# Seven-multiplication projections of a macaron decoder block: products that add up in one PSUM bank, two column pairs in alternation, and another order of pools

## Chip, cores and metric

The kernel runs on one core of a Trainium2 chip, as one launch. The metric is the device time of an execution in microseconds; lower is better. The profile is taken of one execution, with the time of every instruction on TensorE (PE), VectorE (DVE), ScalarE (ACT), GpSimd (POOL) and of the DMA issues on SyncE (SP).

## What is computed

A decoder block over 1024 positions of width 1024, all in float32: a SwiGLU feed-forward stage with half weight, a token mixer, a second feed-forward stage, a final norm. Cut to what matters here:

```python
def swiglu(h, w_in, w_out):
    a, b = jnp.split(h @ w_in, 2, axis=-1)          # 1024 x 1024 by 1024 x 5632
    return (jax.nn.silu(a) * b) @ w_out             # 1024 x 2816 by 2816 x 1024

h = rms_norm(x, norm_ffn1[l]) * (1.0 + sc1) + sh1
x = x + FFN_RESIDUAL * g1 * swiglu(h, ffn1_w_in[l], ffn1_w_out[l])
h = rms_norm(x, norm_mix[l]) * (1.0 + sc2) + sh2
x = x + g2 * token_mixer(h, ..., mix_w_in[l], ...)   # begins with h @ mix_w_in
h = rms_norm(x, norm_ffn2[l]) * (1.0 + sc3) + sh3
x = x + FFN_RESIDUAL * g3 * swiglu(h, ffn2_w_in[l], ffn2_w_out[l])
```

The shifts, scales and gates come from nine modulation vectors, each a product of the conditioning vector with a 1024 x 1024 block of `ada_w`.

## The kernel before

**Matmuls.** A float32 operand is kept as two float32r tiles, a high part (`parts`: an ACT cast, L90) and a low part (a subtraction, L91, on DVE or, for the first weights of a stage, on POOL). A product term is three matmuls of 128 x 128 by 128 x 512: high by high, high by low, low by high (`mmw`, L232 to L234).

**Seven products.** `paired` (L242) computes the projections h @ w_in of the two FFN stages (20 iterations each) and part of that of mix (14 iterations). An iteration takes one pair of column blocks. The weights form a 2 x 2 block matrix (a11, a12 in the tile `ra`, a21, a22 in `rb`), the activations another (b11, b21, b22 and the sums t1 to t4, made once per stage on POOL). Seven block products of 12 matmuls each (`product`, L298) take the place of eight; sums and differences of weights are formed on DVE in `prepare` (L302) and split into the operands w11, w12, w22, ws1 to ws4 in the pool `wp`, 11 tiles. `prepare` of an iteration runs during the iteration before. The pools `hq` and `bq` hold t2, t3 and t4, `hp` the other operands.

Each of the seven products has a PSUM bank of its own, in turn from the pools `pa` and `pb` (four banks each). ACT copies the first bank to a tile (L321); DVE adds the others onto it in seven additions (L323 to L335), in tiles of the pool `cq` ("c"). `emit` follows for each half: `swiglu` in the FFN stages (an ACT Silu and a DVE product), `mix_in` in mix.

**Around it.** In FFN1 `between` (L741) computes the modulation vectors for later: four per iteration in 14 iterations, each a load of 512 KB (`ada`, through the pool `rp` of three buffers, which `ra` and `rb` use too) and a DVE instruction of 128 x 1024 (L154). In both FFN stages `combos` forms the operands of the second product from finished pairs and stores them to DRAM (`bd`, L369).

**Second product.** After `paired`, `ffn` multiplies by w_out, again with seven products, each over eleven blocks and four banks (L432). An operand comes from DRAM: a load into `br` (L404), a cast and a split into `ob`; the weights come through `ar` and `oa`. The pools of this stage (`s1q`, `s2q`, `uq`, `oa`, `ob`, `br`, L393) take the space that `wp` and the others of `paired` have left, in the order in which they are named; so a tile's first writer waits for the last reader of what lay there. The tiles of the following stage of mix (its `wp`, then a unit's weights `wh` and `wl`, L93 to L98) in turn lie on those.

The order on each engine follows the priorities of a tile scheduler: program order, shifted by `defer`. Each engine takes its instructions in that order and waits in place. PE runs the products of an iteration in program order. The change to `paired` starts at L260:

```python
self.part(ctx, wp=11, hq=8, bq=4)
```

Of the kernel before, what the change touches and what calls it, by code (L numbers as in the profile page):

```python
# [22 lines left out]
NKK = 11  # L23
# [17 lines left out]
class Block:  # L41
# [19 lines left out]
    @contextmanager  # L61
    def defer(self, n):

        keep = self.tc.cur_priority
        self.tc.cur_priority = keep + n
        yield
        self.tc.cur_priority = keep

# [160 lines left out]
    def mmw(self, ps, w, i, x, first, last):  # L229
        wh, wl = w[:, 0, i * P:(i + 1) * P], w[:, 1, i * P:(i + 1) * P]  # L230
        mm = self.nc.tensor.matmul
        mm(ps, wh, x[:, 0, :], start=first, stop=False)  # L232
        mm(ps, wh, x[:, 1, :], start=False, stop=False)  # L233
        mm(ps, wl, x[:, 0, :], start=False, stop=last)  # L234
# [7 lines left out]
    def paired(self, ctx, h, hctx, src, order, warm, emit, after, right, ready=()):  # L242


        nc = self.nc
# [4 lines left out]
        def tt(dst, a, b):  # L250
            V.tensor_tensor(dst, a, b, op=sub)
# [8 lines left out]
        self.part(ctx, wp=11, hq=8, bq=4)  # L260
# [26 lines left out]
        for i in range(4):  # L287
            x11, x12, x21, x22 = h[0][i], h[1][i], h[0][4 + i], h[1][4 + i]
            for o, x, y in ((x11, x12, x11), (x12, x22, x12), (x22, x22, x11), (x21, x21, x22)):
                nc.gpsimd.tensor_tensor(o, x, y, op=sub)  # L290
            t2.append(hq(x22))
            t3.append(hq(x12))
            t1.append(self.parts(x11))
            t4.append(self.parts(x21, self.bq, "bq"))
# [18 lines left out]
        ops = None  # L313
        for n, f in enumerate(order):
            if f not in fs:
                w11, w12, w22, ws1, ws2, ws3, ws4 = ops if ops else prepare(f)
                ops = prepare(order[n + 1]) if n + 1 < len(order) else None
                p1, p2, p3, p4, p5, p6, p7 = [self.acc() if (7 * n + i) % 2 == 0 else self.bank() for i in range(7)]
                product(p1, w11, b11)
                c11, c21, c22, u = (self.piece() for _ in range(4))  # L320
                A.copy(u, p1)  # L321
                product(p2, w12, b21)
                V.tensor_tensor(c11, p2, u, op=add)  # L323
                product(p3, ws2, t2)
                V.tensor_tensor(u, p3, u, op=add)
                product(p4, ws3, t3)
                V.tensor_tensor(c22, p4, u, op=add)
                product(p5, w22, t4)
                V.tensor_tensor(c21, p5, c22, op=add)
                emit(f, 0, c11, c21, c21)  # L330
                product(p6, ws1, t1)
                V.tensor_tensor(c22, p6, c22, op=add)
                V.tensor_tensor(u, p6, u, op=add)
                product(p7, ws4, b22)
                V.tensor_tensor(u, p7, u, op=add)  # L335
                emit(f, 1, u, c22, c22)
            after(n, f)
# [6 lines left out]
    def ffn(self, h, hctx, w_in, w_out, gate, warm, residual, norm, done, between=None):  # L344
# [6 lines left out]
        gs = {f: [] for f in order}  # L351
# [4 lines left out]
        def swiglu(f, hh, a, b, dst):  # L356
            s = self.half()
            if dst is None:
                dst = self.half()
            A.activation(s, a, AF.Silu)  # L360
            V.tensor_tensor(dst, b, s, op=ALU.mult)
            gs[f].append(dst)

        def combos(i):

            (x11, x12), (x21, x22) = gs[i], gs[NKK + i]
# [12 lines left out]
            put(6, c4)  # L379
# [12 lines left out]
        with ExitStack() as ctx:  # L392
            self.part(ctx, s1q=11, s2q=11, uq=4, oa=4, ob=3, br=5)  # L393
            self.part(rctx, right=True, xp=8)
            xt, xs = self.xtiles()
            for hh in range(2):
                for i in range(4):
                    nc.sync.dma_start(xt[hh][i], residual(hh, i))
# [47 lines left out]
            b = product(self.acc, lambda i: block(i, 0), 0)  # L446
            us = []
# [227 lines left out]
    def run(self):  # L675
# [113 lines left out]
        def mix_in(f, hh, x, y, dst):  # L789
            sx = x if dst is not None else self.half()  # L790
            A.activation(sx, x, AF.Sigmoid)
            if f >= NH:
                sy = y if dst is not None else self.half()
# [3 lines left out]
            elif f in CONV_EARLY:  # L797
                if hh == 0:
                    us[f] = self.role("u")
# [220 lines left out]
```

## Time and profile before

| quantity | before |
|---|---|
| time, three runs | 2473.93, 2474.76 (median), 2480.92 us |
| profiled execution | 2474.77 us, span of its instructions 2473.0 us |
| PE busy | 2411.6 us, 98% of the span |
| DVE busy | 2012.1 us, 81% |
| ACT busy | 943.4 us, 38% |
| POOL busy | 115.9 us, 5% |
| mean granted PE clock | 0.994 of full speed |
| HBM | 266.31 MB read, 78.12 MB written |

Stages of the span: FFN1's paired stage ends at 484 us and its second product at 700; the first part of mix ends at 1014, the mixer's further parts at about 1810; FFN2's paired stage ends at 2245. A busy time counts instructions that execute; matmuls overlap, so the time between two starts, not the length of one, is what a matmul costs. "idle before <-X" on a row is the time for which the engine stood still ahead of it and what ended that. A window's row gives its length, the busy time of PE, PEld (PE's weight loads), DVE, ACT and POOL in that stretch, with their instructions, and the granted clock (1.00 is 2.4 GHz, 0.50 is 1.2 GHz).

### The profile page before, as it was taken

How to read it: one execution, taken by the hardware profiler on the slowest of the kernel's cores; microseconds unless marked ns; L12 is line 12 of the kernel's file. 1: busy time of each engine (PE TensorE's matmuls, PEld its weight loads, DVE VectorE, ACT ScalarE, POOL GpSimd, SP SyncE). 2: the span in 40 equal slices, each digit the busy share in tenths (PEclk: the TensorE clock that was granted, in tenths of full speed). 3: DMA queues.
4: the chain of work that ended last, by engine and by line, in shares of the span. 5: the costliest groups of instructions: out<-in, count | busy, mean ns of one | idle time of the engine just before them, and what ended most of it. 6: DMA issues, size and time to landing. Idle time of an engine off the chain costs nothing.

```text
span 2473.0 us, 30875 instructions
## 1 busy us (share of the span) xinstructions
PE 2411.6 (98%) x11320; PEld 2002.2 (81%) x11320; DVE 2012.1 (81%) x3010; ACT 943.4 (38%) x1679; POOL 115.9 (5%) x77
## 2 busy tenths in 40 slices
PE   4999999999999999999999999999999999999997
PEld 2788878888878888788888888888888888888886
DVE  8989899678889999799999877575668777775977
ACT  4522233344644333333333335453343333324443
POOL 3300000000060000000000000000050000000000
PEclk9999999999999999999999999999999999999999
DMA  7256565595523323211111112674523233328743
GB/s 276 67 189 209 196 208 187 175 340 179 168 85 119 107 78 113 94 64 61 60 43 64 56 56 82 232 265 157 159 81 124 90 107 106 103 86 291 273 130 124
DMA packets 139975, 346.46 MB, mean 140 GB/s; under 512 B 15536, under 2 KB 15664, under 8 KB 139824
## 3 DMA queue, kind: packets, MB, share of 16 engines
q1 hardware_dynamic: 139680, 343.97, 41.3%
q8 instruction: 89, 1.46, 0.2%
q10 hardware_dynamic: 144, 0.52, 0.1%
q14 instruction: 62, 0.51, 0.1%
HBM read 266.31 MB, written 78.12 MB: 139 GB/s over the span
## 4 chain that ended last, share of the span: by engine, by line
PE 90%; DVE 6%; DMA 2%; issue 1%; ACT 1%; POOL 0%; SPq 0%; DVEq 0%; ACTq 0%
PE pa L233 10%; PE pa L234 10%; PE pa L232 10%; PE pb L234 10%; PE pb L233 10%; PE pb L232 9%; PE pa L106 8%; PE pa L104 8%; PE pa L105 8%; PE pb L577 4%; DMA ada<-in_ada_w_dram 1%; DVE ada L154 1%; PE pb L616 1%; PE pb L601 1%; PE pb L636 1%
## 5 line engine op out<-in xcount | busy, mean ns | idle before, releaser
L90 ACT CAST w<-ra 128x512 fp32r<-128x512 f32 x402 | 238.4, 619 | 435.6 <-PE pb L234 120.0
L104 PE MATMUL pa<-h,wh 128*128 128x512 f32 x896 | 355.4, 397 | 1.5 <-ACT wh L90 1.5
L106 PE MATMUL pa<-h,wl 128*128 128x512 f32 x896 | 353.7, 395 | 1.8 <-DVE wl L91 1.8
L105 PE MATMUL pa<-h,wh 128*128 128x512 f32 x896 | 353.1, 394 | 0.0
L543 DVE SCALAR_TENSOR_TENSOR uc<-u,par,uc 128x1023 f32<-128x1023 f32 (+14 forms) x240 | 303.2, 1263 | 2.7
L91 DVE TENSOR_TENSOR w<-ra,w 128x512 fp32r<-128x512 f32 x378 | 255.0, 690 | 10.6 <-ACT w L90 9.4
L232 PE MATMUL pa<-h,w 128*128 128x512 f32 x504 | 198.4, 396 | 5.0 <-ACT h L90 3.4
L234 PE MATMUL pb<-h,w 128*128 128x512 f32 x504 | 198.0, 393 | 4.7 <-POOL w L91 4.7
L233 PE MATMUL pa<-h,w 128*128 128x512 f32 x504 | 199.2, 395 | 2.7 <-DVE h L91 2.7
L234 PE MATMUL pa<-h,w 128*128 128x512 f32 x504 | 198.1, 393 | 0.0
L106 PEld LDWEIGHTS pa<-h,wl 128*128 128x128 f32 x896 | 168.6, 188 | 36.2 <-DVE wl L91 2.5
L233 PE MATMUL pb<-h,w 128*128 128x512 f32 x504 | 197.5, 392 | 0.0
L104 PEld LDWEIGHTS pa<-h,wh 128*128 128x128 f32 x896 | 168.7, 188 | 35.3 <-ACT wh L90 2.3
L232 PE MATMUL pb<-h,w 128*128 128x512 f32 x504 | 196.3, 390 | 0.0
L105 PEld LDWEIGHTS pa<-h,wh 128*128 128x128 f32 x896 | 168.9, 188 | 33.1 <-issue 0.7
L90 ACT CAST ob<-br 128x512 fp32r<-128x512 f32 x154 | 95.7, 622 | 186.2 <-PE pb L234 80.1
L90 ACT CAST wh<-raw 128x1024 fp32r<-128x1024 f32 x80 | 84.0, 1052 | 207.2 <-PE pa L105 194.4
L91 DVE TENSOR_TENSOR ob<-br,ob 128x512 fp32r<-128x512 f32 x154 | 106.7, 694 | 64.8 <-ACT ob L90 64.1
L233 PE MATMUL pa<-ob,oa 128*128 128x512 f32 x352 | 137.4, 390 | 1.3 <-DVE ob L91 1.3
L232 PE MATMUL pa<-ob,oa 128*128 128x512 f32 x352 | 137.0, 389 | 0.0
L234 PE MATMUL pa<-ob,oa 128*128 128x512 f32 x352 | 137.0, 389 | 0.0
L360 ACT ACTIVATE s<-c 128x512 f32<-128x512 f32 x80 | 50.6, 633 | 186.1 <-DVE c L335 128.3
(233 smaller groups left out, 5035.2 us busy)
## 6 DMA issues: line engine op xcount, KB each, us to landing
ra<-in_ffn_w_in_dram SPq DMA_DIRECT2D x88, 512.0 KB, 4.2
br<-bd SPq DMA_DIRECT2D x154, 256.0 KB, 3.1
bd<-c SPq DMA_DIRECT2D x146, 256.0 KB, 2.0
ada<-in_ada_w_dram SPq DMA_DIRECT2D x72, 512.0 KB, 4.5
ar<-in_ffn_w_out_dram SPq DMA_DIRECT2D x88, 256.0 KB, 4.5
ra<-in_mix_w_in_dram SPq DMA_DIRECT2D x32, 512.0 KB, 3.7
raw<-in_mix_w_in_dram SPq DMA_DIRECT2D x32, 512.0 KB, 3.5
ar<-in_ffn_w_out_dram SPq DMA_DIRECT2D x22, 512.0 KB, 5.2
```

The lines of the kernel that those rows point to most:

```text
L90: self.nc.scalar.copy(hi, src)
L91: (eng or self.nc.vector).tensor_tensor(lo, src, hi.bitcast(F32), op=ALU.subtract)
L104: mm(ps, wh, x[:, 0, :], start=first, stop=False)
L105: mm(ps, wh, x[:, 1, :], start=False, stop=False)
L106: mm(ps, wl, x[:, 0, :], start=False, stop=last)
L154: self.nc.vector.scalar_tensor_tensor(raw, raw, 1.0, self.cs, op0=ALU.mult, op1=ALU.mult, accum_out=dst)
L232: mm(ps, wh, x[:, 0, :], start=first, stop=False)
L233: mm(ps, wh, x[:, 1, :], start=False, stop=False)
L234: mm(ps, wl, x[:, 0, :], start=False, stop=last)
L360: A.activation(s, a, AF.Silu)
L543: V.scalar_tensor_tensor(uc[:, j:], u[:, :S - j], cw(KC - 1 - j), uc[:, j:], op0=ALU.mult, op1=ALU.add)
L577: mm(ps[:, i * 64:(i + 1) * 64], ch(k, i), two(ch(qa, i))[:, :, 1, :], start=True, stop=True)
```

## The change

- `paired`: two iterations are interleaved. A bank `chain` takes w11 b11, then ws2 t2, then (during the next iteration) ws3 t3 and w22 t4, each product added on top of what is there; ACT copies the bank's state after the first (p1) and the second (u2). A bank `low` takes ws1 t1 (copied as p6), then ws4 b22. A bank `left` takes w12 b21. Three DVE additions are left: c11 = left + p1, c12 = low + u2, c22 = chain + p6; the fourth output is read from `chain` itself by `emit`. In the last iteration the order ends with ws4, ws3 (`third`), w12 (`second`), w22 (`fourth`).
- Pools: `wp` has 9 tiles, w22 a pool of 2 of its own; the t's are made in the order t1, t2 and t3, t4; `prepare` makes its operands in another order.
- `ffn`: the pools of the second product are opened in the order `uq, br, ob, s2q, oa, s1q`; the residual x is loaded after the first of its seven products.
- `gs` holds the halves by index, and `mix_in` reuses `y` as the place of its sigmoid only for the second half.

```diff
-        self.part(ctx, wp=11, hq=8, bq=4)
+        self.part(ctx, wp=9, w22=2, hq=8, bq=4)
...
-        def product(ps, w, xs):
-            for i in range(4):
-                self.mmw(ps, w, i, xs[i], i == 0, i == 3)
+        def product(ps, w, xs, more=False):
+            for i in range(4):
+                self.mmw(ps, w, i, xs[i], not more and i == 0, i == 3, more)
 
         def prepare(f):
...
-            w11, w12, w22 = wop(a11), wop(a12), wop(a22)
+            w11, w22 = wop(a11), self.parts(a22, self.w22, "w22")
             V.tensor_tensor(a22, a21, a22, op=add)
+            ws1, w12 = wop(a22), wop(a12)
             tt(a21, a11, a21)
             tt(a11, a22, a11)
+            ws2 = wop(a11)
             tt(a12, a12, a11)
-            ws2, ws3, ws1, ws4 = wop(a11), wop(a21), wop(a22), wop(a12)
+            ws4, ws3 = wop(a12), wop(a21)
...
+        def up(dst, src):
+            with self.sooner(200):
+                A.copy(dst, src)
+
+        def third(chain, ws3, t3, p6, c12, c22, f):
+            product(chain, ws3, t3, True)
+            with self.sooner(200):
+                V.tensor_tensor(c22, chain, p6, op=add)
+            emit(f, 1, c12, c22, c22)
+
+        def fourth(chain, w22, c11, n, f):
+            product(chain, w22, t4, True)
+            emit(f, 0, c11, chain, c11)
+            after(n, f)
...
-                p1, p2, p3, p4, p5, p6, p7 = [self.acc() if (7 * n + i) % 2 == 0 else self.bank() for i in range(7)]
...
+            def second():
+                left = self.bank()
+                product(left, w12, b21)
+                V.tensor_tensor(c11, left, p1, op=add)
+
+            product(chain, w11, b11)
+            up(p1, chain)
+            if old:
+                third(*old[0])
+            product(low, ws1, t1)
+            up(p6, low)
+            if not last:
+                second()
+            product(chain, ws2, t2, True)
+            up(u2, chain)
+            if old:
+                fourth(*old[1])
+            product(low, ws4, b22, True)
+            V.tensor_tensor(c12, low, u2, op=add)
+            old = (chain, ws3, t3, p6, c12, c22, f), (chain, w22, c11, n, f)
+            if last:
+                third(*old[0])
+                second()
+                fourth(*old[1])
...
-            self.part(ctx, s1q=11, s2q=11, uq=4, oa=4, ob=3, br=5)
+            self.part(ctx, uq=4, br=5, ob=3, s2q=11, oa=4, s1q=11)
```

How the instructions stand, at three places. The order of SP where FFN1's paired stage gives way to the second product, before (`ar` are loads of w_out, `br` loads of the stored operands, `bd` stores of them; behind a row, the semaphores that it waits for):

```order
L409 DMA ar_709_4228<-in_ffn1_w_out_dram 128x512 [waits DMAHW1_49,DVE_49]
L404 DMA br_675_4035<-bd00_210 128x512 [waits DMAHW2_49,PE_49]
L404 DMA br_679_4057<-bd01_211 128x512 [waits DMAHW3_49]
L369 DMA bd110_231<-c_646_3882 128x512 [waits DMAHW4_49,DVE_49]
L404 DMA br_683_4079<-bd02_212 128x512 [waits DMAHW5_49]
```

and with the change:

```order
L447 DMA ar_694_4256<-in_ffn1_w_out_dram 128x512 [waits DMAHW5_49,PE_49]
L410 DMA bd210_242<-c_606_3765 128x512 [waits DMAHW6_49,DVE_49]
L442 DMA br_636_3951<-bd00_210 128x512 [waits DMAHW7_49,PE_49]
L442 DMA br_640_3973<-bd01_211 128x512 [waits DMAHW0_49]
L410 DMA bd510_275<-c_612_3894 128x512 [waits DMAHW1_49,DVE_49]
```

The first `br` load waits for a count of PE's matmuls in both; before it is that of the end of the product of w22, the fifth of the last iteration's seven, now that of the end of `second`, the last but one. The loads behind it follow on the same queue.

The order of DVE at the end of mix's paired stage, before (L335 is the last addition of the stage, `msk` are the masks of the units to come, `wl` is the low part of a unit's weight):

```order
L335 TENSOR_TENSOR c_1397_8301<-pb_1393_8285,c_1397_8301 128x512
L828 CAST msk_8431<-rawmask_8432 128x128
L830 CAST msk_8431<-rawmask_8432 128x512 x5
L91 TENSOR_TENSOR wl_1420_8488<-raw_1418_8485,wh_1419_8487 128x1024
```

and with the change (L373 is c12, L335 c22, L358 c11 of `second`):

```order
L373 TENSOR_TENSOR c_1335_8135<-pb_1330_8130,c_1334_8134 128x512
L335 TENSOR_TENSOR c_1336_8136<-pa_1329_8129,c_1332_8132 128x512
L358 TENSOR_TENSOR c_1333_8133<-pb_1337_8237,c_1331_8131 128x512
L95 TENSOR_TENSOR wl_1361_8367<-raw_1359_8364,wh_1360_8366 128x1024
L95 TENSOR_TENSOR wl_1366_8429<-raw_1364_8426,wh_1365_8428 128x1024
L869 CAST msk_8310<-rawmask_8311 128x128
L871 CAST msk_8310<-rawmask_8311 128x512 x5
```

The first two `wl` stand ahead of the masks now, and behind the addition of `second`, the last product but one. On ACT, the cast of the first `wh` waits for the last product before, and for that of ws4 now.

The order of ACT where FFN1's second product ends and mix begins, before (`oa`, `ob` are operands of that product, `w` those of mix's first pair, `s` squares for the norm of the second half):

```order
L90 CAST oa_1040_5890<-a12_1039_5887 128x512
L90 CAST w_1049_5962<-ra_1047_5958 128x512
L90 CAST ob_1042_5895<-br_1041_5893 128x512
L90 CAST w_1050_5965<-ra_1047_5958 128x512
L90 CAST w_1051_5968<-ra_1048_5960 128x512
L90 CAST w_1052_5971<-ra_1048_5960 128x512
L90 CAST w_1055_5978<-ra_1053_5974 128x512
L90 CAST w_1056_5981<-ra_1053_5974 128x512
```

and with the change:

```order
L94 CAST ob_1003_5819<-br_1002_5817 128x512
L214 ACTIVATE s_1025_5932<-x_626_3938 128x512
L214 ACTIVATE s_1026_5935<-x_626_3938 128x512
L214 ACTIVATE s_1027_5938<-x_627_3939 128x512
L94 CAST w_1011_5889<-ra_1009_5885 128x512
L94 CAST w_1012_5892<-ra_1009_5885 128x512
L94 CAST w_1013_5895<-ra_1010_5887 128x512
L94 CAST w_1014_5898<-ra_1010_5887 128x512
```

The casts of `w` stood among the last operands of the product; now they stand behind the last of them and behind three squares, and the third, `w_1013`, waits for the last matmul of the product. POOL's low parts of the same tiles follow these casts in both.

## Rows read from the trace of the kernel before

**Rows 1.** The page: busy times, chain, casts (busy us, mean ns | idle).

```profile
PE 2411.6 (98%) x11320; PEld 2002.2 (81%) x11320; DVE 2012.1 (81%) x3010; ACT 943.4 (38%) x1679; POOL 115.9 (5%) x77
...
PE 90%; DVE 6%; DMA 2%; issue 1%; ACT 1%; POOL 0%; SPq 0%; DVEq 0%; ACTq 0%
...
L90 ACT CAST w<-ra 128x512 fp32r<-128x512 f32 x402 | 238.4, 619 | 435.6 <-PE pb L234 120.0
```

**Rows 2.** Windows of FFN1: busy us (count), clock, DMA share, GB/s.

```profile
124.00:186.00 62.00, 62.00 (x275) 51.36 (x274) 55.41 (x93) 16.08 (x29) 0.00 (x0) 1.00 0.58 187
...
310.00:372.00 62.00, 60.94 (x265) 49.11 (x265) 57.95 (x99) 18.40 (x33) 0.00 (x0) 1.00 0.62 204
372.00:434.00 62.00, 61.08 (x268) 49.91 (x267) 58.79 (x98) 20.32 (x36) 0.00 (x0) 1.00 0.55 187
434.00:478.00 44.00, 44.00 (x195) 36.41 (x194) 29.01 (x47) 13.51 (x24) 0.00 (x0) 1.00 0.43 138
```

**Rows 3.** Groups on DVE, 124 to 434 us (busy, mean ns | idle).

```profile
L154 DVE SCALAR_TENSOR_TENSOR ada<-ada,cs 128x1024 f32<-128x1024 f32 x56 | 68.4, 1221 | 20.6 <-DMA ada<-in_ada_w_dram 20.4
...
L323 DVE TENSOR_TENSOR c<-pa,c 128x512 f32<-128x512 f32 x8 | 5.5, 683 | 0.0
```

**Rows 4.** Waits of PE, 300 to 400 us; timeline at one (start, us).

```profile
PE pa L232 <- ACT c L321: 1.5, 2, 0.8
...
348.77 1.66 ACT L90 CAST w<-ra 128x512 fp32r<-128x512 f32 x3 [1.97 <-DVE ra L251]
350.33 0.58 ACT L321 COPY c<-pa 128x512 f32<-128x512 f32 x1
```

**Rows 5.** Windows at the end of mix (columns as in rows 2).

```profile
1010.00:1014.00 4.00, 3.73 (x17) 2.76 (x15) 3.65 (x7) 2.54 (x6) 0.00 (x0) 1.00 0.29 113
1014.00:1018.00 4.00, 2.24 (x7) 1.34 (x8) 4.00 (x9) 2.32 (x3) 0.00 (x0) 1.00 0.84 245
```

**Rows 6.** Timeline at mix's end: the first unit weight.

```profile
1013.81 1.04 ACT L90 CAST wh<-raw 128x1024 fp32r<-128x1024 f32 x1 [1.15 <-PE pb L234]
...
1014.50 1.76 DVE L830 CAST msk<-rawmask 128x512 uint8<-128x512 f32 x5
1016.18 2.35 DVE L91 TENSOR_TENSOR wl<-raw,wh 128x1024 fp32r<-128x1024 f32 x2
```

**Rows 7.** Timeline where FFN1's second product begins (SPq: SyncE's queue).

```profile
478.23 0.39 PE L232 MATMUL pa<-h,w 128*128 128x512 f32 x1
...
482.94 1.38 ACT L90 CAST ob<-br 128x512 fp32r<-128x512 f32 x2 [6.08 <-DMA br<-bd]
...
483.67 0.43 PE L232 MATMUL pa<-ob,oa 128*128 128x512 f32 x1
```

**Rows 8.** Timeline where FFN2's second product begins.

```profile
2239.50 0.39 PE L232 MATMUL pa<-h,w 128*128 128x512 f32 x1
...
2243.95 1.31 ACT L90 CAST ob<-br 128x512 fp32r<-128x512 f32 x2 [6.66 <-DMA br<-bd]
```

**Rows 9.** Loads of `br`: the page, and landing in 470 to 500 us.

```profile
br<-bd SPq DMA_DIRECT2D x154, 256.0 KB, 3.1
...
DMA to landing us min/median/max: 3.7/4.5/9.8
```

**Rows 10.** Timeline where mix begins: POOL and PE.

```profile
695.42 4.24 POOL L91 TENSOR_TENSOR w<-ra,w 128x512 fp32r<-128x512 f32 x3
...
690.14 0.50 PE L233 MATMUL pa<-ob,oa 128*128 128x512 f32 x1 [1.04 <-DVE ob L91]
...
696.85 0.39 PE L232 MATMUL pa<-h,w 128*128 128x512 f32 x1
...
703.36 1.21 PE L188 MATMUL pb<-ones,s 128*128 128x1 f32 x8 [2.95 <-DVE s L211]
```

**Rows 11.** Windows behind the second of these waits (columns as in rows 2).

```profile
703.00:706.00 3.00, 2.64 (x12) 2.35 (x13) 2.31 (x6) 0.20 (x1) 0.00 (x0) 0.69 0.43 173
706.00:709.00 3.00, 3.00 (x12) 2.37 (x11) 1.93 (x9) 0.00 (x0) 0.00 (x0) 0.74 0.02 5
```

More of the change, by code (lines that the diff above doesn't have):

```diff
@@ L67, in defer, with sooner @@
         self.tc.cur_priority = keep
+    def sooner(self, n):
+        return self.defer(-n)
     def half(self):
@@ L227, in parts, with mmw @@
         return t
-    def mmw(self, ps, w, i, x, first, last):
+    def mmw(self, ps, w, i, x, first, last, more=False):
         wh, wl = w[:, 0, i * P:(i + 1) * P], w[:, 1, i * P:(i + 1) * P]
+        kw = {"skip_group_check": True} if more else {}
         mm = self.nc.tensor.matmul
-        mm(ps, wh, x[:, 0, :], start=first, stop=False)
-        mm(ps, wh, x[:, 1, :], start=False, stop=False)
-        mm(ps, wl, x[:, 0, :], start=False, stop=last)
+        mm(ps, wh, x[:, 0, :], start=first, stop=False, **kw)
+        mm(ps, wh, x[:, 1, :], start=False, stop=False, **kw)
+        mm(ps, wl, x[:, 0, :], start=False, stop=last, **kw)
     def paired(self, ctx, h, hctx, src, order, warm, emit, after, right, ready=()):
@@ L311, in prepare @@
             return w11, w12, w22, ws1, ws2, ws3, ws4
-        ops = None
-        for n, f in enumerate(order):
-            if f not in fs:
-                w11, w12, w22, ws1, ws2, ws3, ws4 = ops if ops else prepare(f)
-                ops = prepare(order[n + 1]) if n + 1 < len(order) else None
-                p1, p2, p3, p4, p5, p6, p7 = [self.acc() if (7 * n + i) % 2 == 0 else self.bank() for i in range(7)]
[L319 to L337, printed above, removed]
@@ new lines, in up @@
+        def up(dst, src):
[10 more added lines that the diff above has]
+            after(n, f)
+        ops, old = None, None
@@ new lines, in paired @@
+        for n, f in enumerate(order):
+            if f in fs:
+                after(n, f)
+                continue
+            last = n + 1 == len(order)
+            w11, w12, w22, ws1, ws2, ws3, ws4 = ops if ops else prepare(f)
+            if not last:
+                ops = prepare(order[n + 1])
+            chain, low = self.acc(), self.bank()
+            p1, p6, c11, u2, c12, c22 = (self.piece() for _ in range(6))
+            def second():
[8 more added lines that the diff above has]
+            up(p6, low)
+            if not last:
+                second()
[10 more added lines that the diff above has]
+                fourth(*old[1])
@@ L350, in ffn @@
         order = [f for i in range(NKK) for f in (i, NKK + i)]
-        gs = {f: [] for f in order}
+        gs = {f: {} for f in order}
         def tt(dst, a, b):
@@ L361, in swiglu @@
             V.tensor_tensor(dst, b, s, op=ALU.mult)
-            gs[f].append(dst)
+            gs[f][hh] = dst
         def combos(i):
-            (x11, x12), (x21, x22) = gs[i], gs[NKK + i]
+            (x11, x12), (x21, x22) = ((gs[j][0], gs[j][1]) for j in (i, NKK + i))
             c3, c2, c4 = (self.piece() for _ in range(3))
@@ L446, in ffn @@
             b = product(self.acc, lambda i: block(i, 0), 0)
+            for hh in range(2):
+                for i in range(4):
+                    nc.sync.dma_start(xt[hh][i], residual(hh, i))
             us = []
@@ L792, in mix_in @@
             if f >= NH:
-                sy = y if dst is not None else self.half()
+                sy = y if dst is not None and hh else self.half()
                 A.activation(sy, y, AF.Sigmoid)
@@ L797, in mix_in @@
             elif f in CONV_EARLY:
-                if hh == 0:
+                if f not in us:
                     us[f] = self.role("u")
```

16 lines of the change are left out of this document (9 added, 7 removed).

## The prediction, made before the change was run

> **What bounds the kernel now.** I read the busy shares and the chain that ended last first. TensorE (PE) is busy 2411.6 us of a span of 2473.0, and 90% of the chain that ended last is PE [rows 1]. The change keeps every matmul, so what it can win is time in which PE stands still, 61.4 us in the whole span, and only those pieces of it that lie where the change works. To see whether a full PE could go faster, I took windows [rows 2]: 275 matmuls in 62.00 us with VectorE (DVE) busy 55.41 us of 62, 195 in 44.00 us with DVE busy 29.01 of 44. That is 0.2255 and 0.2256 us per matmul: DVE's load does not move PE's rate. A product of 12 matmuls is therefore 2.71 us, an iteration of seven 18.9 us, before and after. Then the list of PE's waits and the timelines of the places where the change moves something gave the pieces below.
>
> **The change part by part.** The sum is made against the profiled execution, 2474.77 us (span 2473.0 and 1.8 around it); the median of the three runs is 2474.76, the same. About 0.3%, or 7.4 us, is what a measurement of this kernel tells from no change.
>
> *Adds and copies.* Each of the 54 paired iterations has four DVE adds fewer, at 0.68 us [rows 3], and two ScalarE (ACT) copies more, at 0.58 us [rows 4]. That is 54 x 4 x 0.68 = 147 us of DVE work removed and 54 x 2 x 0.58 = 63 us of ACT work added, nearly none of it on the path. In the FFN1 stage, where DVE also does four 1.22 us modulation products (`mod`) per iteration [rows 3], DVE falls from 57.95 [rows 2] to about 49 us per 62 us window (3.3 iterations x 4 x 0.68 = 9.0). PE shows waits only late there: 62.00 - 60.94 and 62.00 - 61.08, together 1.98 us [rows 2]. Two of them, 1.5 us, are for the copy of a bank [rows 4]: the next product into that bank could not begin, because the copy came late on ACT, behind casts that DVE had held up (1.97 us of idle before them). With the adds gone and a bank of the chain read three products before it is written again (8.1 us for a copy of 0.58), I count **-2.0**. Bounds: 0 if other DVE work stays late, -2.0 if all of it goes. In FFN2 and in mix no such wait exists, so there this part is worth nothing: the cover is PE itself.
>
> *End of mix.* PE stood (4.00 - 3.73) + (4.00 - 2.24) = 2.03 us between 1010 and 1018 [rows 5], waiting for the first plain weight: its cast at 1013.81 had waited 1.15 us for the last matmul of the last product (its buffer lay on that product's operand), and its low part on DVE stood behind the mask casts [rows 6]. In the new order the cast waits for the product of ws4, which ends three products (8.1 us) before the stage does, and the low part stands right behind the add of `second`, ahead of the masks: the add comes 2.7 us before the end, add and split cost 0.7 + 1.2 us, so both are ready 0.8 us ahead of PE. **-2.0** (bounds 0 and -2.0). The price of the split is that of the two `wl` in the rows, 2.35 us for two, 1.2 each; the masks cost 1.76 [rows 6].
>
> *From the paired stage into the second product, twice.* The pools of the second product now lie in another order, so the first `br` load lies on an operand of w12 and must wait for `second`, which is now the last product but one. Before, it waited for the fifth of seven, with two products behind it. The chain from there is in the rows: in FFN1 the next product began at 478.23, the cast of what the load brought began on landing at 482.94, and the first matmul followed at 483.67 [rows 7]: 5.44 us, exactly hidden by 24 matmuls. Now one product hides 2.71 of it: +2.73. In FFN2 the product began at 2239.50, the cast at 2243.95 [rows 8], and with the same 0.73 us from cast to matmul the chain is 5.18 us: +2.47. Together **+5.2**. Nearest bounds: the median `br` load of the kernel lands in 3.1 us [rows 9] where those at the FFN1 place took 4.5 in the middle [rows 9], which would make each stall 1.3 to 1.4 us, +2.7 together; and the second load, queued behind a store on SP, could add 1 us each. I take the rows of the place itself. SP is not held by anything else: its loads of `w_out` are issued ahead.
>
> *Start of mix.* Before, two waits: 1.04 us at 690.14, for an operand's low part that DVE made while GpSimd (POOL) ran those of the weights beside it, and 2.95 us at 703.36 for the norm of the second half [rows 10]. Now the buffers of the warm weights lie on `uq`, `br` and `ob`, which serve to the end of FFN1's second product: the casts stand behind the last operand cast on ACT, the third of them waits for that product's last matmul, and POOL starts its low parts only then. At 4.24 / 3 = 1.41 us each [rows 10] the third low part is ready about 4.24 + 0.35 us (lead of cast and semaphores) after the end, while PE has 7 matmuls (1.6 us) to do before it needs it: 3.0 us of new wait. The norm's result, 6.5 us after the end of the product before, then comes no later than PE. -1.04 - 2.95 + 3.0 = **-1.0** (bounds: -4 if the low parts are early, +3 if the norm's wait remains beside it).
>
> *The residual loads* after the first product lie outside every wait that I see: nothing.
>
> *The clock.* After the 2.95 us wait at 703 the granted clock falls to the 1.2 GHz level for part of 703 to 709: means 0.69 and 0.74 [rows 11], which is 0.31 x 3 + 0.26 x 3 = 1.7 us lost. After the 1.76 us of waiting at 1014 to 1018 it stays at 1.00 (2.4 GHz) [rows 5]. The new waits of 2.73 and 2.47 us lie between these two, nearer the one with a fall. I take one fall of the two: **+1.7** (bounds 0 and +3.4).
>
> Sum: -2.0 - 2.0 + 5.2 - 1.0 + 1.7 = +1.9, so 2474.77 + 1.9 = **2476.7 us**. Much work removed, almost no time moved.
>
> A rule speaks against the change. What the row shows: a copy of a bank takes 0.58 us, and PE waited for such a copy only where ACT reached it late [rows 4]. The Trainium skill, "Perfetto Trace Analysis", section Optimizing Tensor Performance (Matmuls), asks that independent groups rotate through different PSUM banks so that the evacuation of one overlaps the next group's matmuls; the change puts three copies per iteration between products of one and the same bank. By that rule the evacuation would lie open, by the rows it lies beside three other products. I go by the rows; copies in the open are a rival below.
>
> **The rivals.**
>
> *Slower: operands late in FFN1.* The w22 operands get a pool of two of their own. The cast of the next w22 must wait until `fourth` has used the old one, the sixth product of an iteration, 16.2 us into it, and a22 is overwritten in place behind it, so ws1, ws2 and ws4 all queue behind that cast. Cast, add, cast and split, 0.62 + 0.68 + 0.62 + 0.68 [rows 1, 3], make ws1 ready at 18.9 us; its product begins at 18.9 + 5.4 = 24.3: a lead of 5.4 us. DVE's queue is in order, and modulations stand in it that wait for loads (20.6 us of idle before 56 of them [rows 3]). If up to four of them, 1.22 us and a wait each, come in between and eat the lead in the 14 iterations with modulations, each slip counts in full: from a mean of 0.53 us (7.4 / 14) it decides, at 1 us it gives about 2490. For it: DVE waits for these loads already. Against: DVE gets 2.7 us per iteration back. 8%.
>
> *Slower: copies in the open.* If each of the 54 x 3 copies held PE for its 0.58 us, +94 us, about 2570; the shortest distance between a copy and the next write of its bank is two products, 5.4 us, in the first and last iterations. 2%.
>
> *Slightly faster: no stall at the transitions.* If the `br` loads are early after all (another buffer released first), the terms +5.2 and +1.7 go: 2474.77 - 5.0 = 2469.8. For it: the median of 3.1 us; against: the wait is on a named product. 17%.
>
> *No effect on waits at all,* that is, DVE's relief is worth nothing, the end of mix still waits, and only the transitions cost: +5.2 - 1.0 + 3.4 = +7.6, about 2482.4, at the edge of slower. 10%.
>
> *Clearly faster:* the change would have to win over 7.4 us, all waits it touches (1.98 + 2.03 + 1.04 + 2.95 = 8.0) and no stall anywhere. 4%.
>
> **How the numbers follow.** The forecast, 2476.7, has the remaining 59%; by the bounds of its terms (landing, clock, norm) it runs from about 2472.5 to 2480.5. The range reaches down to the case without stalls and up to the case without gains: 2469.5 to 2482.5; outside it lie the two slower rivals and the clearly faster one, 14%, and a little of the edges. Faster by over 0.3% (below 2467.3): 4%. Slower by over 0.3% (above 2482.2): 8 + 2 + a third of the 10 = 13%. Within: 83%.
>
> **What would show it.** Right: DVE's busy time about 1865 us (2012 - 147), ACT's about 1006; PE full in the windows of 310 to 434; a PE wait of 2 to 3 us for `ob` at the start of each FFN's second product; one of about 3 us in two pieces for POOL's low parts at the start of mix, and none for the norm there; none at the start of the units. Wrong: PE waits that repeat every 18.9 us in FFN1 (operands late), waits for the copies, no waits at the two transitions, or a PE rate other than 0.2255 us per matmul.

## The result and the profile after

The changed kernel takes 2495.41 us (median of four runs, 2493.48 to 2496.54) against 2474.35 for the kernel before (four runs, 2473.4 to 2480.92): 0.85% slower, ratio 1.0085, 95% interval 1.0073 to 1.0097. The forecast was 2476.7, 1.9 us slower, with a range of 2469.5 to 2482.5: the sign came true, but the loss is eleven times the one forecast and lies outside the range. The profiled execution is the fastest of the four (2493.48, span 2491.7), so the account below is of 2491.7 - 2473.0 = 18.7 us.

The page after, its busy times, the chain and two groups:

```profile
PE 2418.2 (97%) x11320; PEld 2005.2 (80%) x11320; DVE 1882.5 (76%) x2794; ACT 991.3 (40%) x1787; POOL 114.6 (5%) x77
...
PE 78%; DVE 13%; DMA 6%; issue 1%; ACT 1%; SPq 0%; POOL 0%; DVEq 0%; POOLq 0%; ACTq 0%
...
L95 DVE TENSOR_TENSOR w<-ra,w 128x512 fp32r<-128x512 f32 x378 | 249.6, 689 | 43.8 <-ACT w L94 41.6
...
L238 PE MATMUL pa<-hq,w 128*128 128x512 f32 x432 | 169.9, 393 | 8.7 <-ACT c L330 8.7
```

DVE lost 129.6 us of work (2012.1 in [rows 1]), ACT gained 47.9, and yet the share of PE in the chain that ended last fell from 90% to 78%: more of the chain runs over other engines and loads. The last row says where the largest piece is: 8.7 us of idle before matmuls that wait for a copy of `chain` (L330 is the copy of `up`). Those waits of PE that are spoken of below (total us, times, longest):

```profile
PE pa L238 <- ACT c L330: 8.7, 3, 4.6
...
PE pa L238 <- ACT ob L94: 3.8, 2, 2.2
...
PE pb L238 <- ACT w L94: 3.2, 2, 2.7
...
PE pa L240 <- POOL w L95: 1.7, 2, 1.0
...
PE pb L240 <- DVE w L95: 0.7, 3, 0.4
```

To place the loss I split both spans at the first matmul of a stage (times of PE's rows; difference to before in brackets):

| stage, up to | before | after |
|---|---|---|
| first matmul of FFN1's second product | 483.67 | 489.93 (+6.26) |
| first matmul of mix | 213.18 | 211.85 (-1.33) |
| first matmul of the mixer's units | 318.05 | 323.94 (+5.89) |
| first matmul of FFN2 | 803.83 | 802.71 (-1.12) |
| first matmul of FFN2's second product | 426.21 | 433.44 (+7.23) |
| end | 228.06 | 229.83 (+1.77) |

**The first iteration of each paired stage** is the largest piece. In FFN2 the copy of the first state of `chain` could have run at 1876.7, when its product ended. ACT's rows and the matmul that waited:

```profile
1879.30 0.62 ACT L94 CAST w<-ra 128x512 fp32r<-128x512 f32 x1 [2.54 <-DMA ra<-in_ffn_w_in_dram]
...
1882.48 1.14 ACT L94 CAST w<-ra 128x512 fp32r<-128x512 f32 x2 [1.03 <-DVE ra L316]
1883.99 0.62 ACT L94 CAST w<-ra 128x512 fp32r<-128x512 f32 x1 [0.37 <-DVE ra L257]
1884.51 0.58 ACT L330 COPY c<-pa 128x512 f32<-128x512 f32 x1
```

```profile
1881.78 0.39 PE L240 MATMUL pb<-h,w 128*128 128x512 f32 x1
1885.14 0.50 PE L238 MATMUL pa<-hq,w 128*128 128x512 f32 x1 [2.98 <-ACT c L330]
```

The copy stands behind casts of the second iteration's weights, of which one waited 2.54 us for a load and others for sums on DVE. It came at 1884.51; PE, with two products between, ran out of work at 1882.16 and stood 2.98 us. The same costs 1.09 us in FFN1 and 4.64 in mix. In steady state ACT makes the copy in time, and no other wait of this kind appears.

**The clock** falls behind such waits (windows; the column ahead of the last two is the granted clock):

```profile
312.00:318.00 6.00, 5.10 (x15) 3.74 (x16) 6.00 (x11) 3.75 (x7) 0.00 (x0) 0.72 0.48 157
763.00:771.00 8.00, 6.45 (x17) 5.07 (x18) 5.17 (x9) 5.14 (x11) 0.00 (x0) 0.57 0.40 125
1886.00:1890.00 4.00, 4.00 (x12) 3.14 (x11) 4.00 (x8) 1.48 (x3) 0.00 (x0) 0.57 0.52 197
2261.00:2267.00 6.00, 5.13 (x16) 4.12 (x17) 2.63 (x5) 2.33 (x4) 0.00 (x0) 0.72 0.99 345
703.00:709.00 6.00, 4.84 (x24) 3.85 (x25) 1.24 (x2) 1.86 (x4) 6.00 (x6) 1.00 0.61 196
```

In the first four stretches the clock is at the 1.2 GHz level for part of the time, which loses 0.28 x 6 + 0.43 x 8 + 0.43 x 4 + 0.28 x 6 = 8.5 us; the fifth shows that the fall at the start of mix [rows 11], 1.7 us, is gone.

**FFN1's weights** come late at several iterations from 272 us on, 3.96 us in all and one fall, although DVE is less busy than in [rows 2]:

```profile
124.00:186.00 62.00, 62.00 (x275) 51.36 (x274) 44.64 (x73) 21.14 (x37) 0.00 (x0) 1.00 0.48 157
...
310.00:372.00 62.00, 59.10 (x252) 47.92 (x252) 49.76 (x84) 20.73 (x38) 0.00 (x0) 0.97 0.62 200
```

The worst of these waits, on DVE, ACT and PE:

```profile
307.90 1.22 DVE L158 SCALAR_TENSOR_TENSOR ada<-ada,cs 128x1024 f32<-128x1024 f32 x1 [2.73 <-DMA ada<-in_ada_w_dram]
...
310.26 0.68 DVE L95 TENSOR_TENSOR w<-ra,w 128x512 fp32r<-128x512 f32 x1
...
311.46 0.68 DVE L316 TENSOR_TENSOR ra<-ra 128x512 f32<-128x512 f32 x1
```

```profile
312.23 1.14 ACT L94 CAST w<-ra 128x512 fp32r<-128x512 f32 x2 [7.08 <-DVE ra L316]
```

```profile
312.90 0.80 PE L238 MATMUL pb<-h,w 128*128 128x512 f32 x1 [2.68 <-ACT w L94]
```

A modulation (L158) held DVE's queue 2.73 us for its load; behind it stand the low part of w22 and the sum in place (L316) on which the cast of ws1 waits, 7.08 us of idle on ACT. Between them, in rows left out here, are two differences of `combos` (L395) and a product of `emit` (L402). All four places at which PE waits (272, 313, 354 and 392 us) lie in iterations that also run `combos`, which is every second one; no run leaves `combos` out. Over 124 to 434 us DVE now waits 42.3 us for these loads where it waited 20.4 [rows 3], with the same work in them:

```profile
L158 DVE SCALAR_TENSOR_TENSOR ada<-ada,cs 128x1024 f32<-128x1024 f32 x56 | 68.4, 1221 | 42.3 <-DMA ada<-in_ada_w_dram 42.3
```

**The transitions.** SP's, ACT's and PE's rows where FFN1's second product begins, to be set beside [rows 7]:

```profile
483.55 1.01 SPq L447 DMA_DIRECT2D ar<-in_ffn_w_out_dram  x2
484.80 1.28 SPq L410 DMA_DIRECT2D bd<-c  x1
486.18 0.89 SPq L442 DMA_DIRECT2D br<-bd  x2
```

```profile
489.25 0.62 ACT L94 CAST ob<-br 128x512 fp32r<-128x512 f32 x1 [2.01 <-DMA br<-bd]
```

```profile
489.93 1.20 PE L238 MATMUL pa<-ob,oa 128*128 128x512 f32 x4 [1.65 <-ACT ob L94]
```

The first `br` load is issued 0.6 us after the end of `second` (485.56) and its cast begins 3.07 us later; 1.65 us of wait, 2.17 in FFN2. What held it in FFN1 is SP's queue: the trace lists no wait of the load itself there. It follows a store that took SP from 484.80 to 486.08, and this follows loads of w_out, of which the one at 483.55 had waited 3.0 us for PE (the third matmul of `second` ended at 483.52). In FFN2 the load had a wait of its own, a short one, and its cast began 4.15 us after its issue at 2257.05. From SP's waits there (total us, times, longest):

```profile
SPq L442 <- PE pb L240: 0.5, 1, 0.5
```

Two stages gained. At the start of mix PE waits 0.63 + 1.02 us for POOL's low parts and 1.83 for the norm's spread (L202), without a fall of the clock; at the start of the units the three waits for a weight, 2.03 us together, are gone, and 0.38 + 0.22 us for parts of the activations are new.

### The profile page after: what moved, and what is told of

It reads as the page before. It is cut to its first block, busy times and chain, and to the rows that moved or that the text cites. A ratio compares the mean times of both kernels' runs of the same rounds, so it can differ in the third digit from the quotient of the medians.

```text
span 2491.7 us, 30419 instructions
## 1 busy us (share of the span) xinstructions
PE 2418.2 (97%) x11320; PEld 2005.2 (80%) x11320; DVE 1882.5 (76%) x2794; ACT 991.3 (40%) x1787; POOL 114.6 (5%) x77
## 4 chain that ended last, share of the span: by engine, by line
PE 78%; DVE 13%; DMA 6%; issue 1%; ACT 1%; SPq 0%; POOL 0%; DVEq 0%; POOLq 0%; ACTq 0%
PE pa L239 9%; PE pa L240 9%; PE pa L238 9%; PE pa L110 8%; PE pa L108 8%; PE pa L109 8%; PE pb L240 6%; PE pb L238 6%; PE pb L239 6%; DMA ada<-in_ada_w_dram 4%; PE pb L618 4%; DVE w L95 2%; DVE ada L158 2%; DVE h L95 2%; DVE ra L257 1%
## 5 line engine op out<-in xcount | busy, mean ns | idle before, releaser
L240 PE MATMUL pb<-h,w 128*128 128x512 f32 x720 | 282.7, 393 | 5.5 <-POOL w L95 4.8
L238 PE MATMUL pb<-h,w 128*128 128x512 f32 x720 | 282.0, 392 | 3.2 <-ACT w L94 3.2
L95 DVE TENSOR_TENSOR w<-ra,w 128x512 fp32r<-128x512 f32 x378 | 249.6, 689 | 43.8 <-ACT w L94 41.6
L239 PE MATMUL pb<-h,w 128*128 128x512 f32 x720 | 281.8, 391 | 0.0
L238 PE MATMUL pa<-hq,w 128*128 128x512 f32 x432 | 169.9, 393 | 8.7 <-ACT c L330 8.7
L240 PE MATMUL pa<-hq,w 128*128 128x512 f32 x432 | 169.8, 393 | 0.0
L239 PE MATMUL pa<-hq,w 128*128 128x512 f32 x432 | 169.6, 393 | 0.0
L240 PEld LDWEIGHTS pb<-h,w 128*128 128x128 f32 x720 | 136.2, 189 | 36.8 <-POOL w L95 5.6
L238 PEld LDWEIGHTS pb<-h,w 128*128 128x128 f32 x720 | 136.4, 189 | 32.3 <-ACT w L94 4.1
L239 PEld LDWEIGHTS pb<-h,w 128*128 128x128 f32 x720 | 136.6, 190 | 28.6
L238 PE MATMUL pa<-ob,oa 128*128 128x512 f32 x352 | 137.2, 393 | 3.8 <-ACT ob L94 3.8
```

What stands on the lines that cost most here:

```text
L95: (eng or self.nc.vector).tensor_tensor(lo, src, hi.bitcast(F32), op=ALU.subtract)
L238: mm(ps, wh, x[:, 0, :], start=first, stop=False, **kw)
L239: mm(ps, wh, x[:, 1, :], start=False, stop=False, **kw)
L240: mm(ps, wl, x[:, 0, :], start=False, stop=last, **kw)
```

## Experiments

Each was timed against the kernel before on the same chip; the profile of each gives the waits. There is one profile of a version, and stages that an edit leaves alone differ from one to the next: FFN1's waits for weights are 3.96 us in the change and 4.0, 2.1, 1.4 and 4.0 in e2, e3, e6 and e11, mix's wait for the first copy 4.64 in the change and 4.68, 3.13 and 3.94 in e2, e6 and e11. A difference of 2 us in one such stage is not by itself an effect of the edit.

**e1: the first copies ahead of the next weights' casts.** One column of the tiles that the second iteration's weights are loaded to is written from p1 first, so the loads, and with them the casts, come behind the copy.

```diff
-        def load(f):
+        def load(f, behind=None):
...
+                if behind is not None:
+                    A.copy(rs[b][:, 0:1], behind[:, 0:1])
...
             up(p1, chain)
+            if not old:
+                ops = prepare(order[n + 1], p1)
```

> The change, but in the first iteration of each paired stage the loads of the second iteration's weights wait for the copy p1 of the chain bank, so that ScalarE makes the copies p1 and p6 ahead of the casts of those weights. Theory A (the first-iteration copies stand in ScalarE's queue behind casts that wait for a load; TensorE waits 1.09 + 4.64 + 2.98 us for them, and clock drops of 6.8 and 3.4 us at half speed follow, 5.1 us): these 8.7 us of waits and the 5.1 us go, about 2480 to 2482 us, unless the later weight loads hold the second iteration. Rival B (the copies only show a lateness that the first iteration's operands have anyway): the wait moves to ws2 or to the second iteration's weights and the time stays near 2494.

Measured 2486.48 us (2484.5 to 2489.7), ratio 1.0048 (1.0033 to 1.0063): 9 us less than the change by the medians, though only 3.8 by the profiled executions, of which this is the slowest of its four and that of the change the fastest. ACT's rows at FFN2's start show the copy in its place, ahead of the casts that wait for a load:

```profile
1876.90 0.57 ACT L332 COPY c<-pa 128x512 f32<-128x512 f32 x1
...
1887.31 0.62 ACT L94 CAST w<-ra 128x512 fp32r<-128x512 f32 x1 [7.99 <-DMA ra<-in_ffn_w_in_dram]
```

Of 8.7 us of waits for copies 0.58 is left, and mix up to the units takes 318.05 us, as before (318.05); the clock stays at 1.00 at the first iterations of mix and FFN2. FFN1 grew, though, to 494.04: waits for weights of 5.2 us there, with a fall of the clock, and a stall of 3.18 us at the transition, with another. The two theories split by stage: A holds in mix and FFN2, B's "the wait moves" in FFN1 and with 1.12 us in FFN2. Why the stall at FFN1's transition is longer is open; e10 against e9 below shows the same, 3.52 against 2.00 us.

**e2: `second` ahead of `third` in the last iteration.**

```diff
             if last:
-                third(*old[0])
                 second()
+                third(*old[0])
                 fourth(*old[1])
```

> The change, but in the last iteration second (w12) runs ahead of third (ws3), so that two products instead of one follow the last reader of w12's tile. Theory A (the first load of the second product waits for that tile: 1.65 us in FFN1, 2.17 us and a clock drop of 1.7 us in FFN2): the two waits and the drop go, about 5.5 us less than the change, near 2488 to 2490 us. Rival B (another tile or a store on the same queue holds the load just as long): no difference from the change, 2494.

Measured 2491.66 us (2490.78 to 2493.77). The waits for `ob` fall to 1.14 and about 0.7 us and FFN2's fall of the clock is gone, but `fourth` now follows `third` in the same bank and waits for the addition that reads it in between, three times 0.78 us:

```profile
PE pa L238 <- DVE c L335: 2.4, 3, 0.8
...
PE pa L238 <- ACT ob L94: 1.1, 1, 1.1
```

A holds in part: 3.75 us by the medians, of 5.5 expected. In FFN1 the load was issued at 481.37, 4.8 us earlier than in the change, and yet its cast began only at 487.94: the early issue brought no early landing, and what held it in between is not shown.

**e3: the change with the old pools. e4: the kernel before with the new pools.** One line each; e4's edit is that of e3 the other way round:

```diff
-            self.part(ctx, uq=4, br=5, ob=3, s2q=11, oa=4, s1q=11)
+            self.part(ctx, s1q=11, s2q=11, uq=4, oa=4, ob=3, br=5)
```

> The change with the pools of the second product in their old order. Theory A (in the interleaved stage the last product reads w22, and with the old order the first load of the second product lies on a tile of w22): the load waits for the very last product, and the stall at each of the two transitions grows from about 2 us to about 5 us; at the start of mix the weights' casts are early again (1.65 us of waits for their low parts go, the wait for the norm comes back): about 4 to 7 us above the change, near 2500. Rival B (the other order of pools itself brings the waits at the transitions): these go and the time falls by 4 to 6 us.

> The kernel before with the new order of pools alone. Theory A (the order of pools is worth little by itself, at the start of mix it puts 1.6 us of waits for low parts in place of 1.04 + 2.95 us and the clock drop there may go): 2470 to 2476 us. Rival B (the pools are a large part of the change's loss): over 2480 us.

e3 took 2499.43 us (2496.68 to 2503.23), e4 2493.51 (2489.23 to 2495.96; ratio 1.0073, 1.0058 to 1.0088). e3 went by theory A: 4.66 + 1.28 and 4.71 + 1.27 us at the transitions, and in FFN1 the load's own wait ended with the last product, at 484.35:

```profile
PE pa L238 <- ACT ob L94: 11.9, 4, 4.7
```

```profile
SPq L442 <- PE pa L240: 0.7, 1, 0.7
```

In e4 I had expected the new order to be nearly free, and theory A fell to rival B. Its waits for `ob`, and SP's rows at FFN1's transition:

```profile
PE pa L232 <- ACT ob L90: 12.4, 4, 5.1
```

```profile
479.87 0.89 SPq L409 DMA_DIRECT2D ar<-in_ffn_w_out_dram  x2
480.81 1.37 SPq L404 DMA_DIRECT2D br<-bd  x3
```

The last product ended at 482.18; the load was issued only 1.4 us before that, behind two loads of w_out, and its cast began at 486.42. The trace lists no wait of this load itself; it came late by its place in SP's queue and by 5.6 us from its issue to the cast. So an order of pools is neither good nor bad by itself: each form of the last iteration has the order that fits it, and either of the other two pairings costs 4.7 to 5.1 us per transition, 1.2 to 1.3 for a later load, and a fall of the clock behind each. In the change, the new order is what keeps the transitions at 1.65 and 2.17 us.

**e5: three modulations per iteration, over 19 iterations. e8: w22 in the pool of the others (11 tiles).**

```diff
-                if n >= 3 and n < 17:
-                    for j, k in later[(n - 3) * 4:(n - 2) * 4]:
...
+                for j, k in later[max(n - 3, 0) * 3:max(n - 2, 0) * 3]:
...
-        self.part(ctx, wp=9, w22=2, hq=8, bq=4)
+        self.part(ctx, wp=11, hq=8, bq=4)
...
-            w11, w22 = wop(a11), self.parts(a22, self.w22, "w22")
+            w11, w22 = wop(a11), wop(a22)
```

> The change, with three modulations per iteration over 19 iterations of FFN1 in place of four over 14. Theory A (FFN1's waits for w operands, 0.15 + 2.68 + 0.22 + 0.55 + 0.36 us with a clock drop of 1.7 us behind the longest, come from modulations that wait for their loads in VectorE's queue ahead of the sums of weights): these go, about 4 to 6 us less than the change, near 2490. Rival B (they come from the pool of two for w22 alone): they stay, 2495.

> The change with w22 in the pool of the other weight operands (11 tiles, as before) in place of a pool of two. Theory A (FFN1's waits come from the modulations): FFN1's waits stay about as they are, 2492 to 2497 us apart from what the moved tiles do at the transitions. Rival B (the pool of two makes the next weights late): FFN1's waits go, about 4 us less.

Both times lie outside what either theory gave. e5 took 2507.78 us (2505.26 to 2515.3): the waits for weights did not go but came at every second iteration up to 480 us, 12.6 us in all:

```profile
PE pb L238 <- ACT w L94: 6.3, 6, 1.5
PE pa L240 <- DVE w L95: 3.3, 1, 3.3
```

e8 took 2511.33 (2510.78 to 2514.36): no waits for w operands in FFN1, as rival B had said, but 15.8 us for copies and additions of the banks, most of them in FFN1, and 12.6 at the transitions. FFN1's, up to 480 us:

```profile
PE pa L238 <- DVE c L335: 8.0, 7, 2.3
PE pa L238 <- ACT c L330: 3.4, 5, 1.1
```

Fewer modulations per iteration did not help, but e5 does not vary their number alone: five loads per iteration in place of six fall into other ones of the three buffers, and the modulations reach up to the stage's last iterations. e8 suggests that the pool of two takes part in the lateness, though the 11.4 us for which PE was held by the banks may hide late weights there; the time says that the pool is worth having.

**e9: the change without modulations. e10: e1 without modulations.** The vectors that they would make are set to zero; nothing else is changed.

```diff
+        for m in self.mods[2:]:
+            nc.vector.memset(m, 0.0)
...
-                    for j, k in later[(n - 3) * 4:(n - 2) * 4]:
-                        self.mod(j, k)
```

> The change without the 56 modulations of FFN1 (their loads and VectorE instructions are left out, the vectors are zero, so every shift, scale and gate from the mixer on is wrong and FFN1's result is not added). Theory A (the loads of the modulations share three buffers and VectorE's queue with the weights of the next iteration, and make these late): the waits for w operands in FFN1 go, and FFN1 up to the second product takes no longer than 483.7 + 1.1 (first copy) + about 2 (transition) us. Rival B (the interleaved order with w22's pool of two makes the operands late by itself): waits of the same kind stay.

> The first copies ahead of the next weights' casts, and no modulations (left out as in e9). Theory A (delaying the second iteration's loads cost FFN1 its lead only because the modulations' loads follow in the same three buffers): no wait for w operands in FFN1, where e1 had 4.8 us of them. Rival B (the later loads themselves cost the lead): waits stay.

e9 took 2488.3 us (2485.56 to 2490.55), e10 2481.85 in its one run. In e9 no wait of PE for a weight is left in FFN1's seven-product iterations; its list of waits from 84 to 480 us is one line,

```profile
PE pa L240 <- ACT c L332: 1.1, 1, 1.1
```

and the stage ends at 483.21, 6.7 us earlier than in the change, within 0.5 us of the kernel before. In e10 one wait of 0.16 us is left (e1 has 5.2 us of them, not the 4.8 of the expectation). So the weights are late only beside the modulations. The edit takes away their loads, these loads' share of the three buffers and 68.4 us of DVE's work at once; which of these makes the weights late is not shown, and where in an iteration they stand I did not vary.

**e6: third ahead of ws4 in the last iteration. e11: e6 with the `br` loads from POOL's queue.**

```diff
-            if not last:
-                second()
+            second()
...
+            if last:
+                product(chain, ws3, t3, True)
+                with self.sooner(200):
+                    V.tensor_tensor(c22, chain, p6, op=add)
             product(low, ws4, b22, True)
...
-                nc.sync.dma_start(r, self.b_dram[n][i])
+                nc.gpsimd.dma_start(r, self.b_dram[n][i])
```

> The change with another last iteration: second in its usual place, third ahead of ws4, fourth last, so that no product follows directly on a read of its bank and the first load of the second product waits for a product long done. Theory A (the stalls at the transitions are the wait of that first load for w12's tile): 1.65 and 2.17 us and the clock drop of 1.7 us go, without the three new waits of 0.78 us that second ahead of third brought; about 5 us below the change, near 2490. Rival B (the load would be held by the next tile or by its place in SyncE's queue): 2494 or more.

> The other last iteration of e6, and the loads of the second product's operands on GpSimd's DMA queue, which nothing else uses there, in place of SyncE's. Theory A (in e6 the first of these loads was issued late because it stood on SyncE behind a load of w_out that waited for a low part on VectorE): the stalls of 2.94 and 2.41 us at the start of the second products fall below 1 us each, 4 to 6 us less than e6, about 2485. Rival B (the tile under the load, or its landing, holds it, or loads from GpSimd land later): the stalls stay at 2 us or more.

e6 took 2490.57 us (2490.13 to 2494.31), but not for the reason given: the stalls at the transitions stayed, 2.94 and 2.41 us, and FFN1 happened to lose less on weights (1.4 us). SP at FFN2's transition tells why:

```profile
2252.85 1.48 SPq L449 DMA_DIRECT2D ar<-in_ffn_w_out_dram  x3
2254.38 1.37 SPq L444 DMA_DIRECT2D br<-bd  x3
```

```profile
SPq L449 <- PE pb L240: 4.5, 9, 2.3
...
SPq L449 <- DVE oa L95: 0.2, 1, 0.2
```

The trace lists no wait of the load itself, but it stood on SP behind three loads of w_out. The first of them waited 2.3 us for PE, where the third matmul of the product of ws4 ended at 2252.82; only the third waited for a low part of `oa` on DVE, 0.2 us, so the reason in e11's expectation has the queue right and the wait wrong. The cast of what the load brought began at 2259.32, 4.94 us after its issue. e11 took that queue away: the waits at the two transitions fell to 0.70 us each, as A said. The time did not: 2494.89 us (2491.85 to 2497.21). The second products, 213.47 and 228.31 us in e6, took 214.91 and 231.81, with waits of 0.53 and 1.80 us for operands. At two places that the edit leaves alone its profile lost more as well: 4.0 us on FFN1's weights (1.4 in e6), and 3.94 us on the first copy in mix with 3.4 us of clock (3.13 and 1.7). The landing of the loads:

```profile
br<-bd POOLq DMA_DIRECT2D x154, 256.0 KB, 3.6
```

**e7: e1, e5's and e6's edits together.**

> The change with all three edits: the first copies ahead of the next weights' casts, the new last iteration, three modulations per iteration. Theory A (the loss of 21 us is the sum of these three places: about 13.8 us at the first iterations, 5.5 at the transitions, 3.7 in FFN1, while the start of mix and the end of mix gain): 2470 to 2474 us, no slower than the kernel before. Rival B (the interleaved products cost something everywhere): over 2478 us.

Measured 2498.27 us (2494.78 to 2498.95): A fell as to the total, through e5's edit: +21.6 us up to FFN1's second product against the kernel before (e5 alone: +20.2). The edits of e1 and e6 without that of e5 were not run together. The other stages fit it better: mix +1.6 where the change has +5.9, FFN2 +3.7 where it has +7.2.

**e12: the interleaved products in mix alone,** with e1's edit; FFN1, FFN2 and the pools as before.

> The kernel before with the interleaved products (and the first copies ahead of the next casts) in the mixer's stage alone; FFN1 and FFN2 and the pools of the second product as before. Theory A (the interleaved form costs only at its first iteration, at the transitions to the second product and beside the modulations; at the end of mix it takes away 2.0 us): 2470 to 2474 us, as fast as the kernel before or a little faster. Rival B (the interleaved form costs something in every iteration): over 2476 us.

Measured 2473.46 us (eleven runs, 2470.73 to 2477.98) against 2474.8 (fifteen, 2471.62 to 2476.26): ratio 0.9998, 0.9989 to 1.0007, no difference. In its profile mix takes 317.39 us up to the units, where it took 318.05 before: 1.18 us less for the first unit's weight, whose waits are gone, and 0.66 more for the norm (3.61 us, 2.95 before). That leaves nothing for the fourteen interleaved iterations as such, which settles rival B of e12 and speaks against that of e7. All waits of PE from 690 to 1025 us:

```profile
PE pb L192 <- DVE s L215: 3.6, 1, 3.6
PE pa L108 <- ACT h L94: 0.3, 1, 0.3
```

No version tried beats the kernel before by more than a measurement can tell.

## Why the prediction was wrong

The account of the 18.7 us, from the rows: first iterations 8.7 us of waits and 3.4 + 1.7 of clock, 13.8; FFN1's weights 3.96 + 1.7 - 1.98 = 3.7; transitions 1.65 + 2.17 + 1.7 - 0.23 (a wait for a low part at 484 before) = 5.3; start of mix 0.63 + 1.02 + 1.83 - 1.04 - 2.95 - 1.7 = -2.2; start of the units 0.6 - 2.03 = -1.4. Sum 19.2; the half microsecond between this and 18.7 is not traced (the mixer's units are 1.1 us shorter than before, other stages some tenths longer).

1. **The step that failed: "nearly none of it on the path" for the copies, and with it the rival "copies in the open".** The forecast had no term for the copies; they cost 13.8 of the 18.7 us. I compared the length of a copy, 0.58 us, with the distance to the next write of its bank, 5.4 us in a first iteration, and never asked what stands ahead of the copy on ACT. [rows 4] had shown it: there the copy was late behind casts too. The rival had the place (the first iterations), a wrong mechanism (the copy's length, in every iteration) and 2%. Shown by e1: with the copies ahead of the casts 0.58 of 8.7 us is left, and the falls of the clock behind them are gone.
2. **"-2.0" for FFN1's waits.** It became +3.7. Relief of DVE was real (the windows of 124 to 310 us show it 6 to 11 us less busy per 62 us than before), but DVE's idle time before the modulations' loads doubled. The rival "operands late" named these waits, with the pool of two and the modulations behind them; they came at every second iteration, not every 18.9 us, and their price was under the point from which I let it decide: 3.96 us over 14 iterations is 0.28 each, not 0.53. That it takes the modulations is shown by e9, that the pool of two takes part is suggested by e8; how the lateness builds up over the iterations stays open.
3. **Transitions, "+5.2".** It was 3.82 us, and the path was only half right. The order of the last iteration does make the load late, but hardly through the wait that I had named: the load's own wait for `second` was nothing in FFN1 and 0.5 us in FFN2. "SP is not held by anything else: its loads of `w_out` are issued ahead" was wrong: they and a store stood ahead on the queue, and they waited for matmuls of `second` themselves. e6 and e11 show how much the queue counts: with the tile free the stalls stay, and with the loads on POOL's queue as well they fall to 0.70 us each. As to the size, the load landed 3.07 us after its issue in FFN1, where I took 4.5 and had the page's median of 3.1 as a bound, and 4.15 us after it in FFN2.
4. **Start of mix, "-1.0".** -0.5 by the waits and -1.7 by a fall of the clock that did not come, which I had not counted. The two pieces for POOL's low parts came (1.65 us for 3.0), the norm's wait went, and a wait for its spread took 1.83.
5. **End of mix, "-2.0".** Right: the waits for the weight went whole; with 0.6 us for the activations it is -1.4.
6. **The clock, "+1.7".** One fall in FFN2's transition came as forecast. Three more came behind the waits that I had not seen.
7. **PE's rate** stayed 275 matmuls per 62 us, and e12 shows nothing lost per iteration. The bound that the gain "is only time in which PE stands still" was right, and so was the size of what could be won; what I missed is what could be lost in the three beginnings of 54 iterations. DVE's and ACT's busy times moved by 129.6 and 47.9 us where the forecast had 147 and 63.

## What to carry to other kernels

When a copy moves between two uses of one bank, compare the distance not with the copy's length but with everything that can stand ahead of it in its engine's queue, and look first at the first iteration, where the queue is full of preparation that waits for loads. When DVE's work shrinks in a stage that also streams loads through few buffers, see whether the idle time before its loads grows by as much. An order of pools is fitted to the order of the last readers: change one, and the other has to be fitted again. Before saying what a load waits for, look at what stands ahead of it on its queue, and at what that waits for.

## What was not expected of the hardware

Whether the clock falls is not told by the length of a wait alone: in e6 2.41 us of waiting at 2257.58 left it at 1.00, in e1 waits of 1.36 and 0.36 us at 272 were followed by a stretch at 0.57.

```profile
2257.00:2260.00 3.00, 0.59 (x4) 0.17 (x2) 2.25 (x5) 0.77 (x3) 0.00 (x0) 1.00 0.93 335
2260.00:2266.00 6.00, 6.00 (x26) 4.98 (x27) 3.76 (x6) 2.14 (x4) 0.00 (x0) 1.00 0.93 305
```

```profile
272.00:275.00 3.00, 1.31 (x5) 0.46 (x3) 3.00 (x6) 1.72 (x4) 0.00 (x0) 1.00 0.94 366
275.00:279.00 4.00, 3.96 (x10) 3.14 (x11) 4.00 (x7) 1.98 (x4) 0.00 (x0) 0.57 0.28 49
```

Loads of 256 KB issued by POOL landed in 3.6 us at the median in e11, where those from SP took 3.0 in e6 and 3.1 before [rows 9], and an issue held POOL's queue 0.54 us.
